# Loading a row-reduction kernel's input in two halves of 64 partitions, one on each of two queues

## Chip, cores and metric

The kernel runs on one core of one Trainium2 chip. The metric is device time in microseconds (us) of one execution. Single figures are medians of the runs of one kernel; runs of a kernel mostly agree within 0.4%. The span in a profile is about 1.3 us shorter than the time of the same run.

## The reference

```python
batch, seq, dim = 32, 512, 1024
x = np.random.randn(batch, seq, dim).astype(np.float32)      # 67.1 MB

def reference(x):
    relu_x = np.maximum(x, 0)
    return np.mean(relu_x, axis=-1).astype(np.float32)       # 32 x 512
```

There are 16384 rows of 4 KB. Each is clamped at zero and averaged. Every byte is read once and almost nothing is written.

## The kernel before

Partition p holds 128 neighbouring rows. They are loaded 16 rows at a time into three buffers, so one load is 128 partitions of 64 KB each, 8.4 MB. Rows are shared between ScalarE (even) and VectorE (odd). The last load is cut into ever smaller pieces, so that little work is left when the last byte lands. The first load is moved ahead of the entry barrier.

```python
NB, BUFS = 16, 3                     # rows per load, buffers
full = J // NB - 1                   # J = 128 rows per partition, full = 7
row_pieces = [8, 4, 2, 1]            # the last 16 rows: pieces of rows ...
col_pieces = [512, 256, 256]         # ... and of the very last row

def load(i, dst, src):
    nc.sync.dma_start(out=dst, in_=src).then_inc(loaded[i], 16)

for t in range(full):
    buf_free(t)                      # SyncE waits until both engines are done with load t - 3
    load(t, bufs[t % BUFS][:, :, :], xr[:, t * NB:(t + 1) * NB, :])
# ... the pieces likewise

def rows(i, xt, lo, n, j0):
    nc.scalar.wait_ge(loaded[i], 16)
    nc.vector.wait_ge(loaded[i], 16)
    for k in range(lo, lo + n):
        j = j0 + k
        done = (dve_row if j % 2 else act_row)(nc, xt[:, k, :], sums[:, j:j + 1])
        # ... the last two of a load tell "act" and "dve", for which buf_free waits
# ... last row split over both engines, scaling by 1/1024, one store of 64 KB
```

## Time and profile before

| | before |
|---|---|
| time, median of 3 runs | 162.33 us |
| span of the profiled run | 161.1 us |
| VectorE, ScalarE busy | 74.3, 69.2 us |
| loading queue's share of 16 engines | 97.3% |
| rate from 4.1 to 150 us | 432 GB/s |
| a 64 KB packet, median | 2.418 us |

To read such a profile, look first at who is busy throughout. Neither compute engine is; the DMA engines are. Then ask whether the idle time of the others is a wait for that resource, and in which stretch of time. The prediction shows the lines. The profile also records every DMA packet with its start, duration, size and queue, though not its engine.

### The profile page before, as it was taken

To read this page: it belongs to the slowest core of one execution; us is meant where nothing else is said; L and a number is where in the kernel's file an instruction comes from. 1 tells how busy PE (TensorE), PEld (TensorE's weight loads), DVE (VectorE), ACT (ScalarE), POOL (GpSimd) and SP (SyncE) were. 2 spreads that over 40 slices of the span, in tenths; PEclk is the share of its full clock that TensorE was granted. 3 is DMA by queue.
4 is the path that set the end of the run, shared out by engine and by line. 5 is a ranking of instruction groups with operands and counts; after the bars stand their busy time and mean duration, and the time that the engine had idled before them with its cause. 6 is when DMAs were issued, how large, how long until landed. Compare 5 with 4: busy or idle time off the path is not lost. (4 is left out here: it accounts for less than half of the span.)

```text
span 161.1 us, 336 instructions
## 1 busy us (share of the span) xinstructions
DVE 74.3 (46%) x132; ACT 69.2 (43%) x131; POOL 1.3 (1%) x8
## 2 busy tenths in 40 slices
DVE  0000049800696008940089400992029900498994
ACT  3000049600694008920089200990029800496974
POOL 1000000000000000000000000000000000000001
DMA  7997997997997998999999999999999999899991
GB/s 260 521 472 309 521 472 309 521 456 325 521 439 342 521 423 358 525 391 391 521 391 391 505 407 391 505 407 391 505 407 391 505 407 391 382 464 391 409 401 52
DMA packets 2162, 67.19 MB, mean 417 GB/s; under 512 B 240, under 2 KB 624, under 8 KB 880
## 3 DMA queue, kind: packets, MB, share of 16 engines
q1 hardware_dynamic: 2160, 67.18, 97.3%
q14 instruction: 2, 0.02, 0.0%
HBM read 67.11 MB, written 0.07 MB: 417 GB/s over the span
## 5 line engine op out<-in xcount | busy, mean ns | idle before, releaser
L20 DVE TENSOR_SCALAR_CACHE_REDUCE rows<-rows 128x1024 f32<-128x1024 f32 x64 | 73.3, 1208 | 84.8 <-DMA rows<-in_x_dram 84.6
L15 ACT ACTIVATE rows<-rows 128x1024 f32<-128x1024 f32 x64 | 66.2, 1036 | 88.2 <-DMA rows<-in_x_dram 88.0
L15 ACT ACTIVATION_READ_ACCUMULATOR rows<-rows 128x1 f32 x64 | 11.9, 187 | 0.0
L20 DVE DVE_READ_ACCUMULATOR rows<-rows 128x1 f32 x64 | 5.3, 83 | 0.0
L15 ACT ACT_TABLE_LOAD x1 | 1.3, 1283 | 1.4 <-PEq L55 1.4
L132 POOL TENSOR_SCALAR res<-sums 128x112 f32<-128x112 f32 (+1 forms) x2 | 0.5, 250 | 155.5 <-DVE rows L20 155.5
L15 ACT ACTIVATE last<-last 128x512 f32<-128x512 f32 x1 | 0.6, 629 | 0.0
L20 DVE TENSOR_SCALAR_CACHE_REDUCE last<-last 128x256 f32<-128x256 f32 x1 | 0.4, 420 | 0.2 <-DMA last<-in_x_dram 0.2
L165 DVE SCALAR_TENSOR_TENSOR last<-last,scale 128x258 f32<-128x258 f32 x1 | 0.4, 428 | 0.1
L117 POOL MEMSET scale<- 128x258 f32 x1 | 0.3, 313 | 1.0 <-POOLq L55 1.0
L155 POOL TENSOR_SCALAR res<-part 128x1 f32<-128x1 f32 x1 | 0.3, 264 | 0.6 <-DVE rows L20 0.6
L15 ACT ACTIVATION_READ_ACCUMULATOR last<-last 128x1 f32 x1 | 0.2, 186 | 0.0
L195 POOL MEMSET const-bfloat16-1.0<- 128x1 bf16 x1 | 0.1, 102 | 0.0
L195 POOL MEMSET const-uint8-127<- 128x1 uint8 x1 | 0.1, 102 | 0.0
L195 POOL MEMSET const-float32-0.0<- 128x1 f32 x1 | 0.1, 99 | 0.2 <-issue 0.2
L195 POOL MEMSET const-float32-1.0<- 128x1 f32 x1 | 0.1, 99 | 0.0
L20 DVE DVE_READ_ACCUMULATOR last<-last 128x1 f32 x1 | 0.1, 83 | 0.0
L165 DVE DVE_READ_ACCUMULATOR last<-last,scale 128x1 f32 x1 | 0.1, 82 | 0.0
## 6 DMA issues: line engine op xcount, KB each, us to landing
rows<-in_x_dram SPq DMA_DIRECT2D x1, 4096.0 KB, 39.1
rows<-in_x_dram SPq DMA_DIRECT2D x1, 2048.0 KB, 43.6
rows<-in_x_dram SPq DMA_DIRECT2D x1, 1024.0 KB, 45.6
rows<-in_x_dram SPq DMA_DIRECT2D x1, 512.0 KB, 46.5
last<-in_x_dram SPq DMA_DIRECT2D x1, 256.0 KB, 46.6
last<-in_x_dram SPq DMA_DIRECT2D x2, 128.0 KB, 46.4
rows<-in_x_dram SPq DMA_DIRECT2D x7, 49.2
out_dram<-res SPq DMA_DIRECT2D x1, 64.0 KB, 1.5
```

The lines of the kernel that those rows point to most:

```text
L15: return nc.scalar.activation(out=src, in_=src, func=ACT.Relu, accum_out=acc)
L20: return nc.vector.tensor_scalar(out=src, in0=src, scalar1=0.0, scalar2=init, op0=ALU.max, op1=ALU.add, accum_out=acc,)
L117: nc.gpsimd.memset(scale[:, :], inv).then_inc(pool, 1)
L132: nc.gpsimd.tensor_scalar(out=res[:, lo:hi], in0=sums[:, lo:hi], scalar1=inv, scalar2=0.0, op0=ALU.mult, op1=ALU.add,)
L155: nc.gpsimd.tensor_scalar(out=res[:, J - 2:J - 1], in0=part[:, 0:1], scalar1=part[:, 1:2], scalar2=inv, op0=ALU.add, op1=ALU.mult,).then_i ...
L165: nc.vector.scalar_tensor_tensor(out=last[:, 768:], in0=last[:, 768:], scalar=0.0, in1=scale[:, :], op0=ALU.max, op1=ALU.mult, accum_out=r ...
L195: nc = _bacc.Bacc("TRN2", target_bir_lowering=False, num_devices=1)
```

## The change

The intent was to let two sequencers issue the loads, and to have both first halves under way before the entry barrier. The core of the diff, with cuts:

```diff
-    def load(i, dst, src):
-        nc.sync.dma_start(out=dst, in_=src).then_inc(loaded[i], 16)
...
+    H = P // 2
+    def issue(engine, half, t):
+        if t >= BUFS:
+            engine.wait_ge(act, t - BUFS + 1)
+            engine.wait_ge(dve, t - BUFS + 1)
+        for i in range(t, t + 1 if t < full else len(loads)):
+            dst, src = loads[i]
+            engine.dma_start(out=dst[half], in_=src[half]).then_inc(loaded[i], 16)
+
+    for t in range(full + 1):
+        issue(nc.sync, slice(0, H), t)
+    for t in range(BUFS):
+        issue(nc.scalar, slice(H, P), t)
...
-        nc.scalar.wait_ge(loaded[i], 16)
-        nc.vector.wait_ge(loaded[i], 16)
+        nc.scalar.wait_ge(loaded[i], 32)
+        nc.vector.wait_ge(loaded[i], 32)
...
     for t in range(full):
         rows(t, bufs[t % BUFS], 0, NB, t * NB)
+        if t + BUFS <= full:
+            issue(nc.scalar, slice(H, P), t + BUFS)
```

The helper that moves the first load ahead of the barrier now does so for SyncE and for ScalarE.

## The prediction

The deciding sum was this: while all 16 engines write to one half of the partitions, a 64 KB packet lasts twice the measured 2.418 us, so 64 x 4.84 + 7 = 316 us. The doubling was assumed; no trace showed a transfer of 64 partitions then. The d of the text is an offset between the starts of two engines, by which I let each of their packets be shorter, 4.84 - d: at 0.6 us that gives 64 x 4.24 + 7 = 278 us, and at a whole packet, 2.42 us, 162 us again. The packets that "repeat within a few ns" are the 880 of 64 KB after the first 16: 83% of them took 2.415 to 2.425 us.

> **What bounds the kernel now.** I read the page first, parts 1 to 4, then the waits of the compute engines and of the issuing queue, then a table of stages, and last the single DMA packets in the trace.
>
> ```profile
> span 161.1 us, 336 instructions
> ...
> DVE 74.3 (46%) x132; ACT 69.2 (43%) x131; POOL 1.3 (1%) x8
> ...
> DMA  7997997997997998999999999999999999899991
> ...
> DMA packets 2162, 67.19 MB, mean 417 GB/s; under 512 B 240, under 2 KB 624, under 8 KB 880
> ...
> q1 hardware_dynamic: 2160, 67.18, 97.3%
> ```
>
> Both compute engines are busy less than half of the span; the one DMA queue in use keeps the 16 DMA engines busy for 97.3% of it. The digits of 7 in the DMA row look like gaps but are an artefact of slices (4 us) hardly longer than a packet; the table by stage shows none:
>
> ```profile
> core 0: us, DVE busy (x) ACT busy (x) POOL busy (x), PEclk, DMA share, GB/s
> 0.00:4.10 4.10, 0.00 (x0) 1.28 (x1) 0.52 (x5) 1.00 0.80 272
> 4.10:150.00 145.90, 65.64 (x115) 60.18 (x115) 0.29 (x1) 1.00 1.00 432
> 150.00:158.80 8.80, 8.13 (x17) 7.74 (x16) 0.48 (x2) 1.00 0.84 343
> 158.80:161.10 2.30, 0.53 (x4) 0.03 (x1) 0.00 (x0) 1.00 0.10 29
> ```
>
> From 4.1 to 150 us the DMA share is 1.00 at 432 GB/s, or 27.0 GB/s for each of 16 engines. The waits say the same from the other side:
>
> ```profile
> ACT rows L15 <- DMA rows<-in_x_dram: 88.0, 10, 19.6
> DVE rows L20 <- DMA rows<-in_x_dram: 84.6, 9, 22.5
> ```
> ```profile
> SPq L99 <- DVE rows L20: 105.7, 5, 29.4
> ```
>
> The compute engines wait 88.0 and 84.6 us for loads. The loading queue waits for buffers too, but with two loads still queued ahead of the one it holds back: a 16-row load lands a median 49.2 us after its issue (page, part 6) although its own bytes take only 8.39 MB / 432 GB/s = 19.4 us. So the queue never runs dry, and the end is set by when the last byte lands (158.8 us) plus 2.3 us of last sums and store. The launch figure, 162.33, is 1.2 us above the span.
>
> The packet records give the grain: 896 packets of 64 KB (one partition of one 16-row load), median 2.418 us each, one after another on an engine. Sixteen of them run at any time; 64 KB / 2.418 us = 27.1 GB/s. The first 16 are slower, 2.9 to 3.5 us, and start between 1.0 and 2.0 us.
>
> [...] No transfer of 64 partitions is in this trace.
>
> [...]
>
> [...] packets on one engine follow each other without overlap (a packet ends within some 20 ns of the next one's start).
>
> [...]
>
> **The change, part by part.** Removed: nothing of the bytes. Each of the 14 loads becomes two of 64 partitions, so there are as many data packets as before (128 per load), of the same size.
>
> Added on ScalarE: 14 issues. One took 0.328 to 0.503 us on SyncE in this trace, so 14 x about 0.4 = 5.5 us of ScalarE's sequencer time (estimate from those durations). ScalarE idles 88.0 us for loads; each new issue stands at the end of a tile, where ScalarE finishes about 0.9 us ahead of VectorE and then idles some 10 us. Price on the path: 0. The activation table load (1.28 us) moves from 1.4 to about 2.2 us; first needed near 22 us: 0.
>
> Added semaphore writes: 14 x 16 = 224 records of 9 ns, over 16 engines 14 x 9 ns = 0.13 us.
>
> Moved at the head: half of the first load goes out on each queue. [...] The most this can give is the stagger of the first packets (1.0 us at most, 0.4 us as a mean) and part of their extra length (3.1 instead of 2.42 us, 0.7 us). I count 0 to -0.8 us.
>
> Moved in the memory: this is the term that decides. [...] a packet lasts 2 x 2.418 = 4.84 us. One engine carries 67.11 MB / 16 = 4.19 MB = 64 packets of 64 KB, so 64 x 4.84 = 309 us against 155 now. With the 162.33 - 155 = 7 us around it, about 316 us. [...] The starts seen before differ by 0 to 1.0 us, so d of 0 to 0.6 gives 64 x 4.24 to 4.84 + 7 = 278 to 316 us. [...]
>
> **The rivals.** (1) The engines stay in step: 278 to 316 us. For it: [...] packets that repeat within a few ns, so nothing obvious breaks the step; and [...] a buffer comes free only when all its packets have landed. (2) They slip out of step: [...] Depending on how fast this happens I expect 165 to 260 us. [...] (3) [...] the engines start already alternating because ScalarE's half reaches some of them first (the 16 first starts come in two bunches, 9 by 1.25 us and 7 from 1.64 us): then 161.5 to 163 us, with the bound, 27 GB/s per engine, unchanged. (4) A true gain would need loads faster than 27.1 GB/s per engine, or a shorter head; the head gives under 1 us (0.5%), and 64 x 2.418 = 155 us stays. Faster than 159.1 us (2%) is almost excluded.
>
> A wait that replaces another, such as ScalarE's issue held back by its wait for VectorE, costs nothing while two other loads are queued; it would matter only if the queue ran dry. One half ahead of the other delays the first sums of a tile, not the last byte.
>
> **Range and chances.** I give (1) 40%, (2) 30%, (3) 29%, (4) 1%. The middles 305, 220 and 162 weigh to 0.40 x 305 + 0.30 x 220 + 0.30 x 162 = 237; I say 240 us, knowing that the distribution has two humps and that 240 is between them. The range has to hold both: 160.5 to 318. Chances: faster 0.01; within 2%: 0.29; slower: 0.70.
>
> **What would show each step right or wrong.** Right: 64 KB packets of twice the length (near 4.8 us at the median), a DMA share still at 1.00 with GB/s near 220 to 250, compute engines with the same busy time and longer waits for loads, queue records split evenly between two hardware queues. For (2): packets long at the start and 2.42 us later, with GB/s rising over the span. For (3): 2.42 us throughout, 432 GB/s in the middle stage. The steps on ScalarE are wrong if its waits for VectorE before an issue stand in the chain that ended last, or if the DMA share falls below 1.00 in the middle. The prediction is wrong as a whole if packets stay at 2.42 us: [...] It would also be wrong the other way if the time goes past 318 us[...].

## More of the kernel before

The runs that are compared by a ratio were in the fast state. A kernel run only once has the state "unknown" by rule, and of such runs I read the profile and large differences only.

## The result, and the profile after

The changed kernel takes 316.5 us (315.61 to 316.62, 4 runs) against 162.31 us (162.04 to 162.63, 4 runs). The ratio is 1.949, with a 95% interval of 1.944 to 1.954. Ratios here are the mean time of one kernel's fast runs over that of the other's of the same rounds, so they are not quite the ratio of the medians.

Parts 1 to 3 of the page of the changed kernel:

```profile
span 314.3 us, 355 instructions
...
DVE 74.3 (24%) x132; ACT 69.3 (22%) x131; POOL 1.3 (0%) x8
...
DMA packets 2386, 67.19 MB, mean 214 GB/s; under 512 B 464, under 2 KB 848, under 8 KB 1104
...
q1 hardware_dynamic: 1264, 33.62, 49.4%
q10 hardware_dynamic: 1120, 33.56, 49.4%
```

The busy times of the compute engines have not moved, and neither has the number of bytes. The load is now split evenly between two hardware queues. Together they still occupy the DMA engines for 98.8% of a span twice as long. The engines are as busy as before, at half the rate.

The table by stage of the changed kernel (columns: stretch and its length, then busy time of VectorE, ScalarE and GpSimd, the granted clock, the DMA share and GB/s):

```profile
4.10:150.00 145.90, 27.62 (x48) 25.99 (x49) 0.00 (x0) 1.00 1.01 216
150.00:300.00 150.00, 39.72 (x69) 36.60 (x69) 0.29 (x1) 1.00 0.98 211
300.00:312.00 12.00, 6.47 (x14) 6.09 (x14) 0.48 (x2) 1.00 0.89 244
312.00:314.30 2.30, 0.50 (x4) 0.01 (x1) 0.00 (x0) 1.00 0.10 29
```

The rate is 216 GB/s where it was 432. The loss is nearly uniform over the run (216 and 211 GB/s in the two long stages). In the packet records the last loaded byte lands 3.1 us before the end, where it was 2.8 us. The waits of the compute engines and of the queue:

```profile
ACT rows L15 <- DMA rows<-in_x_dram: 239.2, 11, 37.9
DVE rows L20 <- DMA rows<-in_x_dram: 237.9, 11, 42.9
```
```profile
SPq L109 <- DVE rows L20: 203.7, 5, 48.9
```

Waits for loads grew by 239.2 - 88.0 = 151 us on ScalarE and 237.9 - 84.6 = 153 us on VectorE. The span grew by 314.3 - 161.1 = 153 us. So all the lost time is loads that land later.

In the packet records a 64 KB packet takes 4.91 us at the median on either queue, where it took 2.418. The 16 engines move in bands (the records name the queue, not the engine): 16 packets of SyncE's queue start between 10.40 and 12.09 us, then 16 of ScalarE's between 15.32 and 17.00 us, then SyncE's again. So all engines are on the lower half, then all on the upper: each engine alternates between the two queues by whole packets. The starts inside a band are spread over 1.7 us, and yet all 880 packets of 64 KB that start between 4 and 275 us take 4.88 to 5.30 us.

### The profile page after: what moved, and what is told of

It is laid out like the page before. It is cut to its first block, busy times and chain, and to the rows that moved or that the text cites. A ratio compares the mean times of both kernels' runs of the same rounds, so it can differ in the third digit from the quotient of the medians.

```text
span 314.3 us, 355 instructions
## 1 busy us (share of the span) xinstructions
DVE 74.3 (24%) x132; ACT 69.3 (22%) x131; POOL 1.3 (0%) x8
## 5 line engine op out<-in xcount | busy, mean ns | idle before, releaser
L20 DVE TENSOR_SCALAR_CACHE_REDUCE rows<-rows 128x1024 f32<-128x1024 f32 x64 | 73.4, 1208 | 237.9 <-DMA rows<-in_x_dram 237.9
L15 ACT ACTIVATE rows<-rows 128x1024 f32<-128x1024 f32 x64 | 66.2, 1035 | 239.2 <-DMA rows<-in_x_dram 239.2
```

What stands on the lines that cost most here:

```text
L15: return nc.scalar.activation(out=src, in_=src, func=ACT.Relu, accum_out=acc)
L20: return nc.vector.tensor_scalar(out=src, in0=src, scalar1=0.0, scalar2=init, op0=ALU.max, op1=ALU.add, accum_out=acc,)
```

## The experiments

The theory, P, is the assumption of the prediction: the partitions that the engines write to at one time decide, and while all 16 are on one half (0 to 63 or 64 to 127), a packet takes twice as long. The rivals: Q, two queues cost each other on an engine; R, the reads of the source collide. Twelve kernels were run. Their edits are shown in the core only; changed semaphore counts, and what else follows from an edit, are cut.

### Two queues, but every transfer spans 128 partitions

```diff
-            engine.dma_start(out=dst[half], in_=src[half]).then_inc(loaded[i], 16)
+            d = 1 if len(dst.shape) == 3 and dst.shape[1] > 1 else len(dst.shape) - 1
+            m = dst.shape[d] // 2
+            cut = (slice(None),) * d + (slice(0, m) if half.start == 0 else slice(m, 2 * m),)
+            engine.dma_start(out=dst[cut], in_=src[cut]).then_inc(loaded[i], 16)
```

> Two queues as in the change, but each load is cut along the rows (columns for one-row pieces), so each transfer still spans 128 partitions. Theory P [...]: the loads run at full rate again, 32 KB packets at 1.21 us, 161 to 163 us. Rival Q (two queues on one engine cost each other): still near 316 us.

It takes 163.29 us against 162.27, ratio 1.0067 (1.0048 to 1.0085). The packets of 32 KB take 1.21 us on both queues. The stage table of this kernel:

```profile
4.10:150.00 145.90, 65.27 (x113) 59.80 (x113) 0.29 (x1) 1.00 1.00 430
```

The full rate is back with two queues, so Q is out. Two queues gain nothing either: the kernel is slower by 0.7%, a small loss that I did not take apart. In the profiles the span is 161.9 us against 161.1, and the last loaded byte lands at 158.8 us against 158.3.

### Two halves, but one queue

```diff
-            engine.dma_start(out=dst[half], in_=src[half]).then_inc(loaded[i], 16)
+            for h in (half, slice(H, P)):
+                engine.dma_start(out=dst[h], in_=src[h]).then_inc(loaded[i], 16)
...
-    for t in range(BUFS):
-        issue(nc.scalar, slice(H, P), t)
```

> The two halves of 64 partitions, both issued on SyncE's queue, one after the other. P: packets near 4.9 us, 310 to 320 us, as with two queues, because the engines pass through the lower half together and then through the upper. Q: 162 to 164 us, packets at 2.42 us.

It takes 328.44 us, ratio 2.02, with packets of 5.12 us at the median. Its stage table:

```profile
4.10:150.00 145.90, 27.62 (x48) 25.27 (x48) 0.00 (x0) 1.00 1.01 209
```

The cut by partitions alone makes the loss, and the second queue had even softened it a little: with two queues, whose packets take turns, a packet takes 4.91 us; with one queue, where an engine should have four packets of a half in a row (64 partitions over 16 engines), it takes 5.12.

### Half the data, into two different sets of 64 partitions

These two give wrong results. Loads 0 to 2 and the pieces are those of the kernel before. Loads 3 to 6 bring only 64 partitions, from the same source rows in both kernels.

```diff
-        load(t, bufs[t % BUFS][:, :, :], xr[:, t * NB:(t + 1) * NB, :])
+        dst, src = bufs[t % BUFS], xr[:, t * NB:(t + 1) * NB, :]
+        if t < BUFS:
+            load(t, dst[:, :, :], src)
+        else:
+            load(t, dst[0:64], src[0:64])      # low_only
+            load(t, dst[32:96], src[0:64])     # mid_only, in its place
```

> Wrong results on purpose. Kernel before, but loads 3 to 6 bring only 64 partitions, source rows of partitions 0 to 63 into partitions 0 to 63. P: packets of those loads near 4.9 us, so a half load takes as long as a whole one, 19.5 us, and the total stays near 162 us. Rival R (the reads of the source collide) says the same. If neither: packets 2.42 us, total near 123 us.

> Wrong results on purpose. As low_only, with the very same source rows, but written to partitions 32 to 95[...]. P: packets 2.42 us, each half load 9.7 us, total 162 - 4 x 9.7 = 123 us or a little more (compute takes 9.2 us a tile). R: packets stay near 4.9 us and the total near 162 us.

The first takes 167.78 us, the second 123.42. One line from the stage table of each, first the lower half, then the middle:

```profile
80.00:100.00 20.00, 9.21 (x16) 8.42 (x16) 0.00 (x0) 1.00 0.98 200
```
```profile
80.00:100.00 20.00, 18.66 (x34) 16.85 (x32) 0.00 (x0) 1.00 0.95 408
```

The DMA share is the same, 0.98 and 0.95, and the rate is 200 against 408 GB/s. All 256 packets of loads 3 to 6 take at least 4.49 us in the lower half (median 5.12); 255 of 256 stay below 2.7 us in the middle (median 2.418). Same source rows, same number of partitions, packets, bytes and queues: only the partitions written to differ. So R is out, and so is the idea that a transfer of 64 partitions is slow as such. The middle line also shows VectorE at 18.66 us of 20: with 64 partitions at full rate the loads come as fast as the engines can sum.

### The lower half again, written by eight engines only

```diff
-            load(t, dst[0:64], src[0:64])                   # low_only
+            for a in (0, 1, 2, 3, 32, 33, 34, 35):
+                load(t, dst[a:a + 29:4], src[a:a + 29:4])   # 8 partitions each
```

> Wrong results on purpose. As low_only (loads 3 to 6 bring source rows of partitions 0 to 63 into partitions 0 to 63), but each such load is eight transfers of 8 partitions, every fourth one, so that only 8 of the 16 engines work [...]. P1 [...]: packets of 2.42 us though half of the engines is idle, a half load takes 19.4 us as in low_only, total 162 to 168 us. P2 (an engine that writes through such a half transfer is slow whatever the others do): packets near 4.9 us, a half load takes 39 us, total near 240 us.

It takes 162.11 us (results wrong). Its stage table:

```profile
80.00:100.00 20.00, 9.21 (x16) 8.42 (x16) 0.00 (x0) 1.00 0.49 213
```

Half of the engines is idle (DMA share 0.49) and the rate is 213 GB/s, as with all sixteen. A packet takes 2.418 us at the median, never over 2.95. So an engine is not slow because it writes to this half. It is slow here when the other eight engines write there as well: 8 engines already deliver all that partitions 0 to 63 took from sixteen. This is what P1 forecast; the later runs show that the number of engines on one half is not the whole story.

### Windows between the lower half and the middle

As `mid_only`, with `dst[28:92]` and with `dst[16:80]`; the results are wrong. Each forecast has two outcomes: first, only some of the engines are slow, so that 32 (or 128) of the 256 packets are long; second, the others are slow too, so that most (or nearly all) packets are long.

> Wrong results on purpose. As mid_only (source rows of partitions 0 to 63), but written to partitions 28 to 91[...] of the 256 packets of loads 3 to 6, 32 take near 4.9 us and 224 take 2.42 us; a load takes 19.4 us all the same, total 162 to 168 us. [...] most packets are longer than 2.42 us.

> Wrong results on purpose. As window_28 but partitions 16 to 79[...] 128 packets near 4.9 us and 128 at 2.42 us, total 162 to 168 us. [...] hardly any packet at 2.42 us.

Window 28 takes 178.63 us, window 16 takes 166.75. Their stage tables, window 28 first:

```profile
80.00:90.00 10.00, 8.72 (x15) 8.42 (x16) 0.00 (x0) 1.00 1.00 400
```
```profile
80.00:100.00 20.00, 9.21 (x16) 8.42 (x16) 0.00 (x0) 1.00 0.96 197
```

In window 28 exactly 32 of the 256 packets take over 4.0 us, two at a time, side by side; 195 stay below 2.7 us. Two engines with four packets in each of four loads make 32, so I infer that two engines are slow there and the others hardly suffer. The window lies only four partitions, an engine's share of such a load, below the middle one, where 255 of 256 packets stay below 2.7 us. The total missed its range. The two engines fall behind, and once the others are on the next whole loads (from 109 us) the two take 6.5 to 8.1 us a packet. That is about three times 2.42. The packet records show seven slow packets of 32 KB as well, which I take for those of a third engine, as they lie end to end (114.0 to 141.6 us). They take 3.60 to 4.06 us each, while the median of all 32 KB packets from 112.5 to 132 us is 1.51 us (1.213 in the kernel before). So three engines are slow together, and the packets of the rest are 25% longer meanwhile. Why is not shown.

In window 16 no packet is below 4.1 us (197 GB/s), so all engines are slow there. That is the second outcome. How this comes about is not shown.

### One queue, with eight engines put four packets behind

```diff
+    for a in range(4):       # 2 MB of needless loads, on eight engines only, before halves_one_queue's loads
+        nc.sync.dma_start(out=bufs[2][64 + a:64 + a + 29:4, :, :], in_=xr[a:a + 29:4, 0:NB, :]).then_inc(ahead, 16)
...
+        if t == 2:
+            nc.sync.wait_ge(ahead, 64)
```

The idea was that eight engines on the upper half and eight on the lower would each have the full rate.

> halves_one_queue (328 us) plus four needless transfers ahead of it, 2 MB in all, which put four 64 KB packets on each of eight engines and none on the other eight[...]. P1: packets go back to 2.42 us after the start; 64 x 2.42 + 4 x 2.42 + 7 = 172 us, nearly twice as fast for more bytes; up to 200 us if the shift is not kept exactly. P2: 335 to 340 us, packets unchanged.

It takes 342.91 us, so the forecast of 172 us was plainly missed. The shift itself is there. One group of eight finishes the first lower half between 26.98 and 27.5 us, the other between 36.4 and 39.3. In between one group is on the lower half and the other on the upper, yet the 30 packets of 64 KB that start from 27 to 37 us take 4.99 to 5.13 us. An offset between engines did not help. The stage table from the middle of the run:

```profile
100.00:140.00 40.00, 9.21 (x16) 8.43 (x16) 0.00 (x0) 1.00 1.01 208
```

The start shows it more sharply. The needless loads go to the upper half. Their eight engines are nearly alone at first: six of their second packets, started from 4.72 to 5.14 us, take 2.43 to 2.68 us. From 6.36 us the other eight begin the lower half. All 18 packets that start from 8 to 16 us then take 5.07 to 5.13 us. So everything is slow here although each half has only eight engines, as the lower one had in `low_eight_engines` (2.418 us a packet), and although the packets just before were fast (2.43 to 2.68 us). The total came close to the 335 to 340 us of P2, but P2's reason, that an engine is slow on such a half whatever the others do, had fallen with `low_eight_engines`.

### Which engines are slow together

The obvious excuse was that I had shifted the wrong engines: the two that are slow side by side in window 28 might both belong to the group of eight. In the forecast that is I; C is that one is in the group and one is not. This kernel, with wrong results, gives load 3 to the group of eight as above, and load 4 the window 28.

```diff
+        if t == 3:
+            for a in (0, 1, 2, 3, 32, 33, 34, 35):
+                load(t, dst[a:a + 29:4], src[a:a + 29:4])
+        elif t == 4:
+            load(t, dst[28:92], src[0:64])
```

> Wrong results on purpose. [...] Load 3 as in low_eight_engines (eight transfers of 8 partitions, so only eight engines work, 8 packets each, 19.4 us), load 4 as in window_28 (partitions 28 to 91[...]), the rest as in the kernel before. The other eight engines pass on to load 4 about 10 to 20 us ahead. C ([...] one is in the group of eight and one is not, as one_queue_shifted took for granted): in load 4 the two never meet; no packet near 4.9 us once the group of eight is on load 4. I (both belong to one group): two packets at a time near 4.9 us, side by side, either while the group of eight is still on load 3 or when it comes to load 4, and the failure of one_queue_shifted is explained by it.

While the group of eight is on load 3 (starts from 59.5 to 78 us) eight packets are long, 4.01 to 4.94 us, and the other 103 have a mean of 2.59 us (3.61 at most). The eight follow one another on two engines. One has four such packets, as many as load 4 gives it, and then short ones, so it is outside the group; the other goes on with long ones, as an engine of the group must with its eight packets of load 3. So the two that are slow together are, by this count of packets, one of each group, as C has it, and for this pair the shift was not on the wrong engines.

C's own sign did not come clean, though. Long packets return after 80 us, and why is not shown. The kernel takes 180.8 us.

### Other halves: the middle on one queue, the outer quarters on the other

```diff
-        issue(nc.sync, slice(0, H), t)
+        issue(nc.sync, (slice(32, 96),), t)
...
-        issue(nc.scalar, slice(H, P), t)
+        issue(nc.scalar, (slice(0, 32), slice(96, P)), t)
```

That packets to the outer quarters take near 4.9 us, like those to a half, was assumed here; no run had shown it.

> The change with other halves: SyncE's queue loads partitions 32 to 95 [...], ScalarE's loads 0 to 31 and 96 to 127 in two transfers [...]. P: SyncE's packets 2.42 us, ScalarE's near 4.9 us, 32 x 2.42 + 32 x 4.9 + 7 = 241 us if all engines stay in step. If only the number of partitions in a transfer counted: both near 4.9 us, 316 us.

It takes 306.26 us in its one fast run (a second run of 314.38 us counts as slow), far above 241. Two lines of its stage table:

```profile
5.00:37.00 32.00, 2.11 (x3) 2.80 (x6) 0.00 (x0) 1.00 1.08 295
...
150.00:230.00 80.00, 18.41 (x32) 16.85 (x32) 0.00 (x0) 1.00 0.99 202
```

It begins at 295 GB/s and decays to 202. Up to 37 us only a middle packet that follows another middle packet takes 2.42 us (16 starts, 17.65 to 18.26 us; 2.418 to 2.520). The other 64 middle packets of that stretch follow an outer one and take 2.61 to 4.10 us, 3.16 at the mean; an outer packet takes 4.86 at the mean. Later the engines are out of step, some on the middle and some on the outer quarters, and the mean of a middle packet from 37 to 230 us is 4.12 us, of an outer one 5.12. So the sum of 2.42 and 4.9 was missed from the start (3.16 + 4.86 = 8.0 us), and the rate fell further as the engines got out of step, the contrary of what I let an offset do in the prediction.

### Packets of 4 KB

```diff
-    bufs = [sbuf(f"rows{b}", P, NB, D) for b in range(BUFS)]
+    bufs = [sbuf(f"rows{b}", P, NB, D + 8)[:, :, :D] for b in range(BUFS)]
```

> The change with rows padded by 32 bytes in the buffers, so that a packet is one 4 KB row and no longer 64 KB[...]. In the last 4 KB loads of the changed kernel a packet took 190 ns where it took 159 before. If that carries over: 155 x 190/159 = 185 us, plus 7 is 192 us. If the size of a packet has no part: near 316 us or above.

> Control for the padded buffers: the kernel before with them. A 4 KB packet took 159 ns there against 2418 / 16 = 151 ns for a sixteenth of a 64 KB one: 5% more loading time, 168 to 171 us.

The change with small packets takes 218.38 us, the control 169.46. Their stage tables, the change first:

```profile
4.10:150.00 145.90, 46.03 (x80) 43.41 (x81) 0.00 (x0) 1.00 1.03 318
```
```profile
4.10:150.00 145.90, 59.76 (x103) 55.06 (x105) 0.00 (x0) 1.00 1.03 413
```

The control is as expected. The change with it loses 29% (218.38 / 169.46) where it lost 95% with 64 KB packets: a 4 KB packet takes 208 ns against 161. I had expected 190 ns and called it the figure of the last 4 KB loads of the changed kernel; their packets have a median of 196 ns and a mean of 207, so I had misread it. These are single runs. The size of a packet has a large part in the loss, but small packets do not remove it. Whether it acts through the time that an engine stays on one half was not tested.

## Why the prediction was right, and where it was not

**The outcome, and what decides it: right.** The range held the time, slower had 0.70, and what came is its first rival, "the engines stay in step: 278 to 316 us", almost to the microsecond at its upper end. The point of 240 us was only a weighted mean between two humps, and missed by 76 us. The DMA share at 1.01, 216 GB/s, packets of 4.91 us and unmoved busy times are the signs that it listed. The lower half against the middle (200 against 408 GB/s, same source rows) shows that the partitions written to decide. Why they decide is not shown.

**The deciding term: right to 2%.** It said 4.84 us a packet; it is 4.91. The excess is repaid by the small packets at the end: the last packets of 64 KB end at 277.2 us and the last load at 311.2, so the last eighth of the bytes took 34.0 us, against 8 x 4.91 = 39.3 at the rate of large packets. That two errors cancel is luck. Nor does the size that fits say why a packet is doubled: that was assumed, and in window 16, which takes partitions of both halves, no packet is below 4.1 us either.

**The offset between engines: wrong.** The assumption that a packet lasts 4.84 - d, with d the offset between the starts of two engines, fell. The last engine of a band starts 0.21 us after the one before it (17.00 and 16.79 us), and any other engine is further from it, so by the formula its packet lasts 4.63 us or less; it took 4.92, and none of the 880 took less than 4.88. The deliberate shift of four packets gave nothing (4.99 to 5.13 us). What took its place is known only in part. In window 28 two engines were slow (over 4.0 us a packet), later three, and the rest were a little slower (1.51 against 1.213 us for 32 KB). In window 16 all were slow (4.1 us or more). Engines out of step did not recover (the middle and outer halves, 202 GB/s). Why the shifted kernel was slow from the moment when all sixteen engines were busy, with eight on each half, stays open. The records do not name the engine of a packet, so the pairs are inferred throughout.

**The head: wrong in sign.** I gave 0 to -0.8 us. The first packets start at 1.32 to 2.70 us where they started at 1.00 to 2.04. Two issues at once took 549 and 556 ns, where SyncE's alone took 377. The rest of the 153 us is in the middle stages, so the head was no cause of it to speak of. The prediction also put the last byte of the kernel before at 158.8 us; its packet ends at 158.3, so 2.8 us follow it and not 2.3. Nothing hangs on that.

**ScalarE's issues: mis-sized, free as said.** I took 0.4 us each; they took 0.47 to 0.85 us. The activation table load came at 3.5 us, not 2.2. Neither is on the path: ScalarE still waits 239.2 us for loads.

**The rivals.** Slipping out of step into full rate did not happen in any kernel. Rival (3), 2.42 us throughout, fell with the first profile (4.91 us). The gain that I almost excluded did not come, and the experiment with two queues and 128 partitions shows that the queues by themselves have none to give (430 against 432 GB/s).

## What to carry to other kernels

Here the loads already occupied all DMA engines (DMA share 1.00), so a second queue had nothing to add, and what decided was which partitions each transfer writes to. Keep every large transfer across all 128 partitions, and cut it along rows or columns when it has to be in pieces (430 GB/s here, against 216 for the two halves). If only 64 partitions are to be had, try the middle ones: 32 to 95 had 408 GB/s here, 0 to 63 had 200.
